# Attention in a hybrid diffusion block: who normalises the probabilities, and who splits weights and turns queries

## The chip, the core and the metric

The kernel runs on one core of one Trainium2 chip. Its engines take instructions each from a queue of its own, in order: TensorE (matmuls; PE in the profile, PEld for its weight loads), VectorE (DVE), ScalarE (ACT), GpSimd (POOL), and SyncE (SP), which only issues DMAs here. The metric is the device time of one execution in microseconds, lower is better.

## The reference

One layer over 512 latent tokens of width 1024 with 256 context tokens. What matters for the change is the attention: 16 query heads in 4 groups, each group with one key and value head of 64 columns. A block of 128 queries sees at most three blocks of 128 latent keys, all 256 context keys and one sink logit, in one softmax.

```python
qx = apply_axial_rope(qx.reshape(B, L, N_HEADS, HEAD_DIM), rope_cos, rope_sin)
...
s_loc = jnp.einsum('bqhgd,bshd->bhgqs', qn, kn).astype(jnp.float32) * ATTN_SCALE
s_ctx = jnp.einsum('bqhgd,bchd->bhgqc', qn, k_ctx).astype(jnp.float32) * ATTN_SCALE
s_loc = jnp.where(valid, s_loc, NEG_INF)
probs = jax.nn.softmax(jnp.concatenate([s_loc, s_ctx, sink_b], axis=-1), axis=-1)
...
return (jnp.einsum('bhgqs,bshd->bqhgd', p_loc, vn)
        + jnp.einsum('bhgqc,bchd->bqhgd', p_ctx, v_ctx))
```

The rotary step is `t1*cos - t2*sin`, `t2*cos + t1*sin` on pairs of columns. Beside the attention the layer has a pooling mixer, sigmoid gates, an output projection and a mixture of 32 experts (top 4 of them for each token), whose weights are most of what the kernel reads.

## The kernel before

All float32 products run as three matmuls of rounded halves. A tensor x is split into hi (x rounded, made by a copy on ScalarE) and lo = x - hi (a subtraction), and x*y becomes hi*hi + lo*hi + hi*lo. The subtraction for a weight is called a **weight difference** here, that for the transposed probabilities a **probability difference**.

The stages are: adaptive norm and key/value projections (to about 105 us), the attention (to about 396 us), pooling mixer, branch projections, output projection and routing (to about 650 us), and the experts, 32 of them with twelve weight pieces of 1 MB each, to the end.

The attention stage is written out by hand in the order in which each engine is to work. It goes over 16 **units** (4 groups x 4 query blocks; unit 0 starts at 118 us), each of six **slots** k = 0 to 5. In a slot:

- TensorE makes the scores of head k (S, two buffers in PSUM), transposes block k of the previous unit's probabilities (tp, two buffers), multiplies an older block with the values (pv), and fills up with `stream()`: 22 projection tiles of 24 matmuls (fps; six query tiles and sixteen gate tiles).
- ScalarE copies the transposed block to ph (`b_hi`, line 529), takes the exponential of head k-1 (`a_exp`, line 518; es of line 520 for the sink), normalises, and rounds weights (`s_split`, line 696).
- VectorE makes the probability difference pl = tp - ph (`b_lo`, line 533), the row maximum of head k (`a_max`, lines 513, 514), and in slots 2 and 4 the reciprocals of two heads at a time (`a_rec`, lines 501, 502).

`a_norm(U, k - 2)` (line 504) multiplies a head's probabilities with the reciprocal of their sum. Heads 0 and 2 follow right on the reciprocal in slots 2 and 4, heads 1 and 3 come in slots 3 and 5. Odd heads are normalised by ScalarE (line 507), even ones by VectorE (line 509). A unit's probabilities are 128 x 512 or 128 x 640 for each head.

Small pieces of work wait in the list `lazy` and are taken out one or two in a slot (`run_lazy(LZN[k])`), after the slot's main work: the output difference, the query's f13 (shuffle, two products, sum) and the query differences. A weight tile is rounded in two halves of 128 x 512 when the tile before it is at its 4th and 10th matmul; the two weight differences `f()` of a tile (line 699) run on GpSimd at once. When the second of a pair is done, the load of the next pair but one is issued. `stream()` doesn't begin a tile before both its differences are in the program.

The rotary step of four tiles ahead of the stage (`roped`, line 206; the last two are the queries of group 0) has one product on GpSimd and one product and the sum on VectorE. The six query tiles of the stage (`q_epi`) have both products and the sum on GpSimd (lines 613, 616, 619).

GpSimd and VectorE also share a third kind of work, **w_ada work**: a conditioning vector times a weight, ten column pieces in the units 0 to 7, 9 and 11. GpSimd does half of a piece in four instructions (lines 633, 635), VectorE the other half in eight running sums of 128 x 128 (lines 640, 642).

Of the kernel before, what the change touches and what calls it, by code (L numbers as in the profile page):

```python
# [10 lines left out]
F32 = mybir.dt.float32  # L11
# [4 lines left out]
AF = mybir.ActivationFunctionType  # L16
ALU = mybir.AluOpType
# [4 lines left out]
L = 512  # L22
# [46 lines left out]
def body(ctx, tc, x, c, cx, c_ctx, w_ada, b_ada, norm1_g, norm2_g, w_in, b_in, attn_sink, w_pool,  # L69
# [4 lines left out]
    pe, dve, act, pool = nc.tensor, nc.vector, nc.scalar, nc.gpsimd  # L74
# [122 lines left out]
    rope = slot("17a", [P, 2 * L], F32, "rope")  # L197
# [8 lines left out]
    def roped(pt, off, m, nm, t=None, t2=None):  # L206
        if t is None:
            t, t2 = wb([P, L], F32, "rope_t"), wb([P, L], F32, "rope_s")
        act.activation(t, pt, AF.Identity, bias=bcol(off, m), scale=1.0)
        dve.stream_shuffle(t2, t, swap)  # L210
        pool.tensor_mul(t, t, rope[:, 0:L])
        dve.tensor_mul(t2, t2, rope[:, L:])
        dve.tensor_add(t, t, t2)
        return t
# [288 lines left out]

    def a_norm(U, h):
        den, prob, W = U["den"], U["prob"], U["W"]
        if h % 2:
            act.activation(prob[:, h, 0:W], prob[:, h, 0:W], AF.Copy, scale=den[:, h:h + 1])
        else:
            dve.tensor_scalar(prob[:, h, 0:W], prob[:, h, 0:W], den[:, h:h + 1], None, op0=ALU.mult)

    def a_max(U, h, S):
        hd, W, nmh = GRP * U["g"] + h, U["W"], U["nm"][:, h:h + 1]
# [79 lines left out]
    def q_epi(g, m):  # L592
        def epi(pt):
            st = {}

            def f0():
                st["t"] = wb([P, L], F32, "rope_t")
                act.activation(st["t"], pt, AF.Identity, bias=bcol(OQ, 2 * g + m), scale=1.0)  # L598
                lazy.insert(0, f13)
                due.extend([(cnt[0] + 4, lambda: f5(0)), (cnt[0] + 5, lambda: f5(1))])  # L600

            def f13():
                f1()
                f2()
                f3()
                f4()

            def f1():
                st["t2"] = wb([P, L], F32, "rope_s")
                dve.stream_shuffle(st["t2"], st["t"], swap)  # L610

            def f2():
                pool.tensor_mul(st["t"], st["t"], rope[:, 0:L])

            def f3():
                pool.tensor_mul(st["t2"], st["t2"], rope[:, L:])

            def f4():
                pool.tensor_add(st["t"], st["t"], st["t2"])

            def f5(par):
                hd = 2 * m + par
                r = slice(par * 64, par * 64 + 64)
                ro = slice(64 - par * 64, 128 - par * 64)
                act.copy(qs_[g][r, hd, :], st["t"][r])
                lazy.insert(min(1, len(lazy)), lambda: dve.tensor_sub(qs_[g][ro, hd, :], st["t"][r],
                                                      qs_[g][r, hd, :].bitcast(F32)))
            post.insert(0, f0)
        return epi
# [57 lines left out]
    def s_split(i, part):  # L687
        if i >= len(tiles):
            return
        r, m, _ = tiles[i]  # L690
        if part == 0:
            wsp[i] = (hw([P, KT, P], F32R, "whi"), hw([P, KT, P], F32R, "wlo"))
        k = slice(4 * part, 4 * part + 4)
        hi, lo = wsp[i]
        src = raws[r][:, k, m * P:(m + 1) * P]
        act.copy(hi[:, k], src)

        def f():
            pool.tensor_sub(lo[:, k], src, hi[:, k].bitcast(F32))  # L699
            if part == 1 and m == 1:  # L700
                s_load(r + 2)
            wdone[i] = wdone.get(i, 0) + 1
        f()

    def stream():
        for i, (r, m, epi) in enumerate(tiles):
# [29 lines left out]
    with tc.manual_schedule():  # L736
# [23 lines left out]
        st = stream()  # L760
# [990 lines left out]
```

## Time and profile before

| what | value |
|---|---|
| median of 3 runs | 1830.98 us (1830.45 to 1831.39) |
| the profiled execution | 1827.51 us, its span 1825.7 us |
| TensorE busy | 1715.2 us, 94% of the span |
| VectorE busy | 1606.9 us, 88% |
| ScalarE busy | 1138.6 us, 62% |
| GpSimd busy | 411.6 us, 23% |
| DMA | 506.13 MB, 277 GB/s over the span |

The shares are means over stages that are bound by different things, so they don't tell what a change in one stage is worth. The views of stretches, groups and single units below are read for that. A duration in the profile holds the time in which an instruction has started but stands blocked; an idle gap before it is listed apart, with what ended it. Durations of neighbours overlap by about a tenth of a microsecond, so the distance from start to start is what an engine pays.

### The profile page before, as it was taken

To read this page: it belongs to the slowest core of one execution; us is meant where nothing else is said; L and a number is where in the kernel's file an instruction comes from. 1 tells how busy PE (TensorE), PEld (TensorE's weight loads), DVE (VectorE), ACT (ScalarE), POOL (GpSimd) and SP (SyncE) were. 2 spreads that over 40 slices of the span, in tenths; PEclk is the share of its full clock that TensorE was granted. 3 is DMA by queue.
4 is the path that set the end of the run, shared out by engine and by line. 5 is a ranking of instruction groups with operands and counts; after the bars stand their busy time and mean duration, and the time that the engine had idled before them with its cause. 6 is when DMAs were issued, how large, how long until landed. Compare 5 with 4: busy or idle time off the path is not lost. (4 is left out here: it accounts for less than half of the span.)

```text
span 1825.7 us, 22699 instructions
## 1 busy us (share of the span) xinstructions
PE 1715.2 (94%) x8398; PEld 1277.2 (70%) x8398; DVE 1606.9 (88%) x1691; ACT 1138.6 (62%) x1209; POOL 411.6 (23%) x260
## 2 busy tenths in 40 slices
PE   5888889999999899999999999999999999999994
PEld 3767777877779767776766777777777777777763
DVE  5589998848886789998999999999999999999994
ACT  5456666763242367775766677677667777776762
POOL 0055445222441011424411111211111121112001
PEclk9998999999999899999999999999999999999997
DMA  9223323234655799999999999999999999999972
GB/s 302 69 84 104 104 87 103 77 121 134 213 179 176 245 304 348 357 376 335 355 367 360 362 376 370 364 368 370 377 364 370 369 372 365 375 367 361 377 283 101
DMA packets 180380, 506.13 MB, mean 277 GB/s; under 512 B 12506, under 2 KB 69094, under 8 KB 180266
## 3 DMA queue, kind: packets, MB, share of 16 engines
q1 hardware_dynamic: 172170, 484.17, 72.7%
q0 software_dynamic: 8096, 20.48, 4.4%
q8 instruction: 67, 1.10, 0.2%
q14 instruction: 47, 0.39, 0.1%
HBM read 490.02 MB, written 22.69 MB: 281 GB/s over the span
## 5 line engine op out<-in xcount | busy, mean ns | idle before, releaser
L1555 DVE TENSOR_TENSOR mwl<-mw,mwh 128x2048 fp32r<-128x2048 f32 x384 | 873.3, 2283 | 37.1 <-PE gu L1285 29.4
L1548 ACT CAST mwh<-mw 128x2048 fp32r<-128x2048 f32 x384 | 727.3, 1911 | 258.6 <-PE dn L1285 118.8
L1285 PE MATMUL gu<-mwh,xT 128*96 128x512 f32 x2048 | 523.1, 398 | 3.0 <-DVE xT L125 2.7
L1285 PEld LDWEIGHTS gu<-mwh,xT 128*96 128x96 f32 x2048 | 327.1, 162 | 139.5 <-DVE xT L125 3.1
L1290 POOL DMA_INDIRECT acc<-y,igs x31 | 121.0, 3904 | 917.1 <-DVE y L1398 917.1
L1285 PE MATMUL gu<-mwl,xT 128*96 128x512 f32 x1024 | 280.1, 396 | 3.0 <-DVE mwl L1555 3.0
L1285 PE MATMUL dn<-mwh,aT 128*96 128x512 f32 x992 | 253.2, 397 | 0.0
L1285 PEld LDWEIGHTS gu<-mwl,xT 128*96 128x96 f32 x1024 | 166.0, 162 | 76.0 <-DVE mwl L1555 3.4
L1285 PEld LDWEIGHTS dn<-mwh,aT 128*96 128x96 f32 x992 | 155.4, 162 | 61.5
L1285 PE MATMUL dn<-mwl,aT 128*96 128x512 f32 x496 | 135.0, 394 | 0.0
L714 PE MATMUL fps<-hx,whi 128*128 128x512 f32 x352 | 124.3, 412 | 3.0 <-ACT rope_t L598 1.9
L1285 PEld LDWEIGHTS dn<-mwl,aT 128*96 128x96 f32 x496 | 79.9, 161 | 34.7
L1375 ACT ACTIVATE gs<-gs 96x1024 f32<-96x1024 f32 x32 | 34.0, 1062 | 88.8 <-DVE gs L1372 88.8
L1246 POOL DMA_INDIRECT xgb<-h2d,igs x31 | 79.9, 2577 | 40.8 <-DVE ltok L1180 16.7
L714 PEld LDWEIGHTS fps<-hx,whi 128*128 128x128 f32 x352 | 68.0, 195 | 19.0 <-ACT rope_t L598 3.0
L714 PE MATMUL fps<-hx,wlo 128*128 128x512 f32 x176 | 71.9, 409 | 0.8 <-POOL wlo L699 0.8
L518 ACT ACTIVATE prob<-S,nm 128x512 f32<-128x512 f32 (+1 forms) x64 | 47.8, 747 | 34.6 <-DVE nm L514 34.1
L533 DVE TENSOR_TENSOR pl<-tp,ph 128x512 fp32r<-128x512 f32 x72 | 49.2, 684 | 8.5 <-ACT ph L529 8.1
L525 PE MATMUL tp<-ident,prob 128*128 128x128 f32 x288 | 45.3, 281 | 11.3 <-DVE pl L533 11.2
L513 DVE TENSOR_REDUCE nm<-S 128x1 f32<-128x512 f32 (+1 forms) x64 | 47.9, 748 | 6.0 <-PE S L488 5.7
L1398 DVE SCALAR_TENSOR_TENSOR y<-dn,gts,g2r 96x512 f32<-96x512 f32 x64 | 44.9, 740 | 5.0 <-PE dn L1285 5.0
L529 ACT CAST ph<-tp 128x512 fp32r<-128x512 f32 x72 | 41.9, 584 | 5.0 <-PE tp L525 4.5
(418 smaller groups left out, 2564.0 us busy)
## 6 DMA issues: line engine op xcount, KB each, us to landing
mw<-in_w_gu_dram SPq DMA_DIRECT2D x256, 1024.0 KB
mw<-in_w_down_dram SPq DMA_DIRECT2D x128, 1024.0 KB
wada<-in_w_ada_dram SPq DMA_DIRECT2D x24, 1024.0 KB
gz<-gzt SPq DMA_DIRECT2D x16, 256.0 KB
sg<-gz SPq DMA_DIRECT2D x16, 256.0 KB
wo<-in_w_out_dram SPq DMA_DIRECT2D x4, 1024.0 KB
xt<-in_x_dram SPq DMA_DIRECT2D x2, 1024.0 KB
xh<-in_x_dram SPq DMA_DIRECT2D x4, 512.0 KB
```

What stands on the lines that cost most here:

```text
L513: dve.reduce_max(nmh, S[:, 0:W], axis=AX.X)
L518: act.activation(U["prob"][:, h, 0:W], S[:, 0:W], AF.Exp, bias=nmh, scale=SCALE, accum_out=U["den"][:, h:h + 1])
L525: pe.transpose(U["tp", j][:, h * P:(h + 1) * P], U["prob"][:, h, j * P:(j + 1) * P], ident)
L529: act.copy(U["ph", j], U["tp", j])
L533: dve.tensor_sub(pl, U["tp", j], U["ph", j].bitcast(F32))
L714: pe.matmul(pt, a[:, k, :], b(k), start=n == 0, stop=n == 3 * KT - 1)
L1246: pool.indirect_dma_start(out=xg, out_offset=None, in_=h2d, in_offset=bass.IndirectOffsetOnAxis(ap=ig, axis=0), bounds_check=L - 1, oob_is ...
L1285: pe.matmul(os_[j], lhs(a, k), b[:, k, j * L:(j + 1) * L], start=first and j not in seen, stop=last and j not in left)
L1290: pool.indirect_dma_start(out=acc, out_offset=bass.IndirectOffsetOnAxis(ap=iscat, axis=0), in_=y, in_offset=None, bounds_check=L - 1, oob_ ...
L1398: dve.scalar_tensor_tensor(st["y"][:, cs], st["dn"][n], st["gt"], g2r[0:CAP, cs], op0=ALU.mult, op1=ALU.mult)
L1548: act.copy(hi, raw)
L1555: eng.tensor_sub(lo, raw, hi.bitcast(F32))
```

## The change

It does three things. All four heads of a unit are normalised by ScalarE. The weight differences of `stream()` go from GpSimd to VectorE, and they no longer run at once but are put at the end of `lazy`. The rotary products and sums go from GpSimd to VectorE. The w_ada work stays as it was.

```diff
--- before.py
+++ after.py
@@ -208,7 +208,7 @@
             t, t2 = wb([P, L], F32, "rope_t"), wb([P, L], F32, "rope_s")
         act.activation(t, pt, AF.Identity, bias=bcol(off, m), scale=1.0)
         dve.stream_shuffle(t2, t, swap)
-        pool.tensor_mul(t, t, rope[:, 0:L])
+        dve.tensor_mul(t, t, rope[:, 0:L])
         dve.tensor_mul(t2, t2, rope[:, L:])
         dve.tensor_add(t, t, t2)
         return t
@@ -503,10 +503,7 @@
 
     def a_norm(U, h):
         den, prob, W = U["den"], U["prob"], U["W"]
-        if h % 2:
-            act.activation(prob[:, h, 0:W], prob[:, h, 0:W], AF.Copy, scale=den[:, h:h + 1])
-        else:
-            dve.tensor_scalar(prob[:, h, 0:W], prob[:, h, 0:W], den[:, h:h + 1], None, op0=ALU.mult)
+        act.activation(prob[:, h, 0:W], prob[:, h, 0:W], AF.Copy, scale=den[:, h:h + 1])
 
     def a_max(U, h, S):
         hd, W, nmh = GRP * U["g"] + h, U["W"], U["nm"][:, h:h + 1]
@@ -610,13 +607,13 @@
                 dve.stream_shuffle(st["t2"], st["t"], swap)
 
             def f2():
-                pool.tensor_mul(st["t"], st["t"], rope[:, 0:L])
+                dve.tensor_mul(st["t"], st["t"], rope[:, 0:L])
 
             def f3():
-                pool.tensor_mul(st["t2"], st["t2"], rope[:, L:])
+                dve.tensor_mul(st["t2"], st["t2"], rope[:, L:])
 
             def f4():
-                pool.tensor_add(st["t"], st["t"], st["t2"])
+                dve.tensor_add(st["t"], st["t"], st["t2"])
 
             def f5(par):
                 hd = 2 * m + par
@@ -696,11 +693,11 @@
         act.copy(hi[:, k], src)
 
         def f():
-            pool.tensor_sub(lo[:, k], src, hi[:, k].bitcast(F32))
+            dve.tensor_sub(lo[:, k], src, hi[:, k].bitcast(F32))
             if part == 1 and m == 1:
                 s_load(r + 2)
             wdone[i] = wdone.get(i, 0) + 1
-        f()
+        lazy.append(f)
 
     def stream():
         for i, (r, m, epi) in enumerate(tiles):
```

What this does to the order is seen in unit 4. VectorE, from the first reciprocal (rec: add of den and es, reciprocal) to the second, before (pl is the probability difference, nm the row maximum, prob the probabilities):

```order
L501 TENSOR_TENSOR den_1674<-den_1674,es_1676 128x2
L502 RECIPROCAL den_1674<-den_1674 128x2
L509 TENSOR_SCALAR prob_1673<-prob_1673,den_1674 128x512
L533 TENSOR_TENSOR pl_1784<-tp_1738,ph_1780 128x512
L513 TENSOR_REDUCE nm_1675<-S_1767 128x1
L514 TENSOR_SCALAR nm_1675<-nm_1675,nsink_92 128x1
L640 TENSOR_SCALAR wada2_1652<-wada2_1652,sil_103 128x128
L533 TENSOR_TENSOR pl_1803<-tp_1773,ph_1799 128x512
```

and after:

```order
L501 TENSOR_TENSOR den_1673<-den_1673,es_1675 128x2
L502 RECIPROCAL den_1673<-den_1673 128x2
L530 TENSOR_TENSOR pl_1783<-tp_1738,ph_1779 128x512
L510 TENSOR_REDUCE nm_1674<-S_1766 128x1
L511 TENSOR_SCALAR nm_1674<-nm_1674,nsink_92 128x1
L696 TENSOR_TENSOR wlo_1763<-ws__1287,whi_1762 128x512
L637 TENSOR_SCALAR wada2_1651<-wada2_1651,sil_103 128x128
L530 TENSOR_TENSOR pl_1803<-tp_1772,ph_1799 128x512
```

Line 509 is gone from behind the reciprocal, so that the probability difference follows it at once; a weight difference stands in front of the w_ada product of the next slot.

ScalarE in the same part of unit 4, from the copy of the second transposed block on, before (ph is the copy of a transposed block, whi a rounded weight half):

```order
L529 CAST ph_1746<-tp_1712 128x512
L518 ACTIVATE prob_1673,den_1674<-S_1706,nm_1675 128x512
L520 ACTIVATE es_1676<-sink_91,nm_1675 128x1
L696 CAST whi_1762<-ws__1222 128x512
L529 CAST ph_1780<-tp_1738 128x512
L518 ACTIVATE prob_1673,den_1674<-S_1732,nm_1675 128x512
L520 ACTIVATE es_1676<-sink_91,nm_1675 128x1
L507 ACTIVATE prob_1673<-prob_1673,den_1674 128x512
L529 CAST ph_1799<-tp_1773 128x512
```

and after:

```order
L526 CAST ph_1746<-tp_1712 128x512
L515 ACTIVATE prob_1672,den_1673<-S_1706,nm_1674 128x512
L517 ACTIVATE es_1675<-sink_91,nm_1674 128x1
L506 ACTIVATE prob_1672<-prob_1672,den_1673 128x512
L693 CAST whi_1762<-ws__1287 128x512
L526 CAST ph_1779<-tp_1738 128x512
L515 ACTIVATE prob_1672,den_1673<-S_1732,nm_1674 128x512
L517 ACTIVATE es_1675<-sink_91,nm_1674 128x1
L506 ACTIVATE prob_1672<-prob_1672,den_1673 128x512
L526 CAST ph_1799<-tp_1772 128x512
```

The normalisation of head 0 now stands in front of the rounded weight and of the third ph; before, ScalarE's first normalisation of the unit was head 1's, one exponential later.

VectorE in the last rotary chain ahead of unit 0, from the query differences of the first query tile to those of the second, before:

```order
L443 TENSOR_TENSOR qs_946<-rope_t_947,qs_946 64x512 x2
L210 STREAM_SHUFFLE rope_s_963<-rope_t_962 128x512
L212 TENSOR_TENSOR rope_s_963<-rope_s_963,rope_93 128x512
L213 TENSOR_TENSOR rope_t_962<-rope_t_962,rope_s_963 128x512
L443 TENSOR_TENSOR qs_946<-rope_t_962,qs_946 64x512 x2
L513 TENSOR_REDUCE nm_977<-S_980 128x1
```

and after:

```order
L443 TENSOR_TENSOR qs_946<-rope_t_947,qs_946 64x512 x2
L696 TENSOR_TENSOR wlo_959<-ws__800,whi_958 128x512
L210 STREAM_SHUFFLE rope_s_963<-rope_t_962 128x512
L211 TENSOR_TENSOR rope_t_962<-rope_t_962,rope_93 128x512
L212 TENSOR_TENSOR rope_s_963<-rope_s_963,rope_93 128x512
L213 TENSOR_TENSOR rope_t_962<-rope_t_962,rope_s_963 128x512
L696 TENSOR_TENSOR wlo_959<-ws__800,whi_958 128x512
L443 TENSOR_TENSOR qs_946<-rope_t_962,qs_946 64x512 x2
L510 TENSOR_REDUCE nm_977<-S_980 128x1
```

The product of line 211 has come over from GpSimd, and two weight differences stand around the chain.

## Rows read from the trace of the kernel before

**Rows 1.** Stretches: busy PE, PEld, DVE, ACT, POOL; TensorE's clock; DMA share; GB/s.

```profile
118.00:264.00 146.00, 124.11 (x668) 101.56 (x669) 138.90 (x257) 91.13 (x204) 83.14 (x66) 0.94 0.28 93
277.00:326.00 49.00, 44.32 (x258) 36.13 (x257) 44.13 (x86) 34.54 (x76) 26.37 (x22) 1.00 0.29 97
326.00:376.00 50.00, 50.00 (x305) 43.13 (x304) 38.47 (x86) 39.56 (x91) 11.85 (x9) 1.00 0.18 64
700.00:750.00 50.00, 50.00 (x233) 35.31 (x232) 49.29 (x36) 35.50 (x24) 10.16 (x3) 1.00 0.99 358
```

**Rows 2.** VectorE groups, 118 to 264 us: busy us, mean ns | idle before.

```profile
L642 DVE SCALAR_TENSOR_TENSOR wada<-wada,sil 128x128 f32<-128x128 f32 x54 | 34.5, 639 | 1.2
L501 DVE TENSOR_TENSOR den<-den,es 128x2 f32<-128x2 f32 x16 | 9.1, 571 | 0.8 <-ACT es L520 0.8
L509 DVE TENSOR_SCALAR prob<-prob,den 128x640 f32<-128x640 f32 x8 | 8.9, 1114 | 0.3
L509 DVE TENSOR_SCALAR prob<-prob,den 128x512 f32<-128x512 f32 x8 | 6.3, 784 | 0.3
L626 DVE TENSOR_TENSOR qs<-rope_t,qs 64x512 fp32r<-64x512 f32 x8 | 8.2, 1025 | 0.2
```

**Rows 3.** The same view, 277 to 326 us.

```profile
L642 DVE SCALAR_TENSOR_TENSOR wada<-wada,sil 128x128 f32<-128x128 f32 x12 | 6.1, 505 | 0.3
L501 DVE TENSOR_TENSOR den<-den,es 128x2 f32<-128x2 f32 x6 | 3.3, 552 | 0.5 <-ACT es L520 0.5
L509 DVE TENSOR_SCALAR prob<-prob,den 128x640 f32<-128x640 f32 x4 | 3.9, 982 | 0.1
L509 DVE TENSOR_SCALAR prob<-prob,den 128x512 f32<-128x512 f32 x2 | 2.4, 1188 | 0.1
```

**Rows 4.** Single lines, whole span: duration ns min/median/max, first and last start us.

```profile
L642 DVE SCALAR_TENSOR_TENSOR wada<-wada,sil x70: 334/352/1991, 132.0 to 328.0; 128x128 f32<-128x128 f32 x70
L501 DVE TENSOR_TENSOR den<-den,es x32: 143/160/1273, 121.6 to 376.7; 128x2 f32<-128x2 f32 x32
L533 DVE TENSOR_TENSOR pl<-tp,ph x72: 672/683/693, 140.2 to 388.8; 128x512 fp32r<-128x512 f32 x72
L626 DVE TENSOR_TENSOR qs<-rope_t,qs x12: 686/751/1686, 148.5 to 326.8; 64x512 fp32r<-64x512 f32 x12
L212 DVE TENSOR_TENSOR rope_s<-rope_s,rope x2: 693/693/693, 106.4 to 112.4; 128x512 f32<-128x512 f32 x2
```

**Rows 5.** GpSimd's weight differences (line 699) in the two stretches.

```profile
118.00:264.00 146.00, 30.68 (x22) 0.94 0.28 93
277.00:326.00 49.00, 9.41 (x8) 1.00 0.29 97
```

**Rows 6.** GpSimd's w_ada work, 118 to 264 us: line 633, then line 635.

```profile
118.00:264.00 146.00, 15.73 (x8) 0.94 0.28 93
...
118.00:264.00 146.00, 20.95 (x24) 0.94 0.28 93
```

**Rows 7.** VectorE, last rotary chain ahead of unit 0: start us, us.

```profile
112.35 0.69 DVE L212 TENSOR_TENSOR rope_s<-rope_s,rope 128x512 f32<-128x512 f32 x1
114.23 1.76 DVE L213 TENSOR_TENSOR rope_t<-rope_t,rope_s 128x512 f32<-128x512 f32 x1 [1.19 <-POOL rope_t L211]
```

**Rows 8.** Unit 4 in order of time: VectorE's rows, then ScalarE's.

```profile
198.75 0.17 DVE L502 RECIPROCAL den<-den 128x2 f32<-128x2 f32 x1
200.76 0.68 DVE L533 TENSOR_TENSOR pl<-tp,ph 128x512 fp32r<-128x512 f32 x1
...
197.22 0.61 ACT L529 CAST ph<-tp 128x512 fp32r<-128x512 f32 x1
199.01 0.72 ACT L507 ACTIVATE prob<-prob,den 128x512 f32<-128x512 f32 x1 [0.32 <-DVE den L502]
199.63 0.57 ACT L529 CAST ph<-tp 128x512 fp32r<-128x512 f32 x1
```

**Rows 9.** Waits of VectorE, 111 to 396 us: us in total, times, longest.

```profile
DVE pl L533 <- ACT ph L529: 8.1, 12, 1.7
```

## The prediction

> **What bounds the kernel now.** I read the profile from the outside in: first busy time by stretch, then the VectorE groups of the stretches the change touches, then one unit of the attention in order of time. The attention stage runs from 118 us, where unit 0 begins, to about 396 us. In its units 0 to 7 (118 to 264 us) and 9 to 11 (277 to 326 us) the busiest engine is VectorE: 138.9 of 146 us and 44.1 of 49 us, 95% and 90%, with TensorE at 85% and 90% and ScalarE at 62% and 70%. In units 12 to 15 (326 to 376 us) it turns round: TensorE is busy all 50 us, VectorE 77%, ScalarE 79% [rows 1]. So there are 195 us in which a microsecond of VectorE is worth about a microsecond, and 50 us in which it is worth nothing. What the attention gains or loses goes through to the end: the later part moves weights at a DMA share of 0.99 with 358 GB/s [rows 1], against 0.18 to 0.29 in the attention, and its loads start as the buffers of earlier stages come free, so a shift of this stage shifts all that follows.
>
> The second thing to see is that VectorE isn't 95% busy with its own work. The running sums of line 642 have a median of 352 ns but a mean of 639 ns in units 0 to 7, and the two-element addition of line 501 has 160 against 571 ns [rows 2, 4]. The probability differences of line 533, just as wide but with one input in PSUM, go from 672 to 693 ns over all 72 of them [rows 4]. So instructions whose operands all lie in SBUF sit blocked behind a GpSimd instruction, and those that read PSUM don't.
>
> **The change part by part.** All sums are made in the profiled execution (1827.5 us, span 1825.7); that is 3.5 us under the median of 1830.98, so I add the difference to the median.
>
> 1. VectorE loses its half of the normalisations: 8.9 + 6.3 us in units 0 to 7 and 3.9 + 2.4 us in units 9 to 11 [rows 2, 3]: -21.5 us, blocked time included.
>
> 2. Blocking given back. Of the other instructions, lines 642, 501 and 626 lose 54 x (0.639 - 0.352) = 15.5, 16 x (0.571 - 0.160) = 6.6 and 8 x (1.025 - 0.686) = 2.7 us in units 0 to 7, and lines 642 and 501 lose 12 x (0.505 - 0.352) = 1.8 and 6 x (0.552 - 0.160) = 2.4 us in units 9 to 11 [rows 2 to 4]: 29.0 us. GpSimd keeps only the w_ada work, lines 633 and 635: 15.7 + 21.0 of its 83.1 us in units 0 to 7 [rows 1, 6]; 56% of its time leaves. By that share 0.56 x 29 = 16 us come back; at most all 29. I take 25, near the upper end, because smaller groups that are blocked too are left out of the 29, and because the first two w_ada runs no longer stand behind weight differences in GpSimd's queue and can run before unit 0. -25 us, from -16 to -29.
>
> 3. VectorE takes over 22 + 8 weight differences [rows 5] and three operations for each of six rotary tiles, 48 instructions of 128x512. An unblocked multiplication of this kind took 693 ns [rows 4]: 48 x 0.69 = +33.1 us. In the 326 to 376 us stretch TensorE covers the rest.
>
> 4. These 48 read SBUF twice, so what is left on GpSimd can block them. Eight of its ten w_ada runs, four instructions each, take 36.7 us in units 0 to 7 [rows 6], so all ten some 46 us of the 195, at 1.15 us an instruction; hit with a chance of 0.24 and held for half of one, the 48 lose 48 x 0.24 x 0.57 = 6.5 us, and nothing where VectorE waits anyway. I take +4, from 0 to 6.5.
>
> The Trainium skill (SBUF - State Buffer, Who interferes with whom) says that a VectorE instruction with two SBUF inputs contends with GpSimd reads, that the one that started first keeps the shared pair for its whole length, and that an instruction with one SBUF input outside a 2-port mode doesn't contend. The trace agrees (line 533 never above 693 ns, line 642 up to 1991). By that rule term 4 is there; if the moved differences were as immune as line 533 is, the sum would be 4 us lower.
>
> VectorE's own load in the 195 us thus goes down by 21.5 + 25 - 33.1 - 4 = 9.4 us.
>
> 5. The new wait. This is where the forecast is decided. Head 0 and head 2 are now normalised on ScalarE, in the very slot in which VectorE makes their reciprocal, and behind them in ScalarE's queue stands the copy of the next transposed block (line 529), for which VectorE's next probability difference (line 533) waits. In unit 4 of before, the reciprocal starts at 198.75 us and VectorE needs the next copy at 200.76; ScalarE had made it at 197.22, before the reciprocal was there [rows 8]. After the change it can't: ScalarE stands still until the reciprocal is done, then normalises (0.62 us from one start to the next in unit 4, for 512 columns), then copies (0.57) [rows 8], with about 0.1 us for two handovers: VectorE gets its input 1.3 us after its reciprocal. In some units a weight copy of half a microsecond stands between (the order of unit 4 shows it); in others VectorE has a weight difference of 0.69 us to fill the hole, in unit 4 none. So the hole after the first reciprocal is 0.6 to 1.9 us. After the second one VectorE has its own work queued (w_ada products, differences, 0.7 to 1.4 us), so that hole is 0 to 1.0. Before, VectorE waited on this copy 12 times for 8.1 us in the whole stage [rows 9]. From 0.6 to 2.9 us a unit, I take 1.5, since the first hole is open nearly everywhere and the second seldom. Unit 0 has no probability differences, so ten units of the VectorE-bound stretches count: +15 us, from 6 to 29.
>
> 6. Start of the stage. In the last rotary chain before unit 0 VectorE waits 1.19 us for GpSimd's product and then its addition takes 1.76 us instead of 0.69, blocked by a weight difference [rows 7]. With all three operations in a row, 112.35 + 2 x 0.70 + 0.69 = 114.4 us instead of 115.99: -1.5 us, from 0 to -2, since ScalarE's casts come next.
>
> 7. The TensorE-bound units. ScalarE's 39.6 of 50 us [rows 1] takes eight more normalisations of some 0.75 us: 45.6, 91%. It has to wait for reciprocals as well. I take half a microsecond a unit, +2 us, from 0 to 5.
>
> Where the weight differences stand in the queue costs nothing: TensorE's wait for GpSimd before a second weight half becomes a wait for VectorE that an earlier probability difference has already met in all but the first tiles. The weight loads are issued behind the second difference, a slot or two later, with a whole pair of tiles still in hand.
>
> Sum: -9.4 + 15 - 1.5 + 2 = +6.1 us. Forecast: **1837 us**, slower by 0.3%.
>
> **The rivals.** (a) The relief passes through, and the kernel gets faster. That is one mechanism: between reciprocal and next difference VectorE always has more than the 1.3 us of work that ScalarE needs. Then the hole is 0.4 us a unit and term 7 is nothing: -9.4 - 1.5 + 4 = -7, that is 1824 us. For it speaks that ScalarE is only 62% busy where VectorE binds [rows 1]; against it, that in the order of unit 4 nothing at all stands there. It decides below about 0.9 us of hole a unit, where the sum crosses zero. The Trainium skill (Perfetto Trace Analysis, Optimizing Scalar/DVE Operations) says that a saturated VectorE may hand work to ScalarE, and that moves between VectorE and GpSimd might not help since they share a port. If the exchange with GpSimd gave nothing either way, -21.5 - 1.5 + 4 = -19 would make 1812 us; but terms 2 to 4 of the rows make that exchange 12 us dearer, so of this rival's chance I give it 0.04.
>
> (b) Both halves cancel: with holes of about 0.5 to 1.2 us a unit, 1831 us within 3.7. That needs only a slightly cheaper handover than mine, or w_ada blocking that falls into the holes.
>
> (c) ScalarE becomes the bound in the TensorE-bound units too, and GpSimd's remaining work blocks the 48 new instructions in full: -21.5 - 16 + 33.1 + 6.5 + 25 + 5 - 1 = +31, 1862 us. Against it: 9% of ScalarE are still free there.
>
> (d) The moved work isn't on VectorE at all, or the normalisations still alternate: the order rules that out.
>
> **How the numbers follow.** Differences within 0.2% (3.7 us) can't be told from none here. Forecast (+3.7 to +20 us) 0.50; rival (a) 0.22; (b) 0.24; (c) 0.04. Faster 0.22, same 0.24, slower 0.54. The ends of the unknown costs together would be about -13 and +36 us; two in ten are left out at 1823 and 1851. The likeliest case alone is 1835 to 1851.
>
> **What would show it.** Lines 642 and 501 with means near 400 and 250 ns confirm term 2. A new row in the waits, probability difference on ScalarE's copy, of 15 to 20 us in all (8.1 now), and ScalarE's normalisation waiting on the reciprocal 25 times or more confirm term 5; if both stay under 8 us, (a) is right. VectorE under 90% with TensorE no busier in units 1 to 7 means the holes are real. I am wrong if units 0 to 7 take less than 140 us, or if units 12 to 15 grow by more than 4 us, or if the later stages don't shift by what the attention does.

## The result: slower by 1.0%

| | before | after |
|---|---|---|
| median of 5 runs each, in one comparison | 1830.45 us (1827.59 to 1831.39) | 1847.89 us (1847.62 to 1850.55) |
| ratio, 95% interval | | 1.0102, 1.0088 to 1.0117 |
| span of the profiled execution | 1825.7 us | 1846.1 us |
| VectorE busy, GpSimd busy, whole span | 1606.9, 411.6 us | 1598.7, 313.4 us |

The forecast was 1837.0 us, with a range of 1823 to 1851. The direction and the range hold; the step is 17.4 us between the medians, not 6.1, and 20.4 us between the two profiled spans, by which the trace is read below. In the changed kernel the lines behind line 506 have moved up by three: the probability difference is line 530 there, ph 526, the row maximum 510, the running sums 639, the normalisation 506, GpSimd's w_ada work 630 and 632. One of the six executions of kernel e5 below took 2158.09 us at a granted clock of 0.745, and its time is the median of the other five.

Below are the stretches that [rows 1] has of before, now of the changed kernel: units 0 to 7, units 9 to 11, units 12 to 15, and 50 us of the experts. The columns are the same (stretch, its length, busy PE, PEld, DVE, ACT, POOL, clock, DMA share, GB/s).

```profile
121.80:268.00 146.20, 122.90 (x667) 99.72 (x668) 120.37 (x274) 101.09 (x220) 28.79 (x24) 0.95 0.28 90
283.00:337.70 54.70, 45.91 (x254) 37.05 (x253) 43.31 (x91) 38.64 (x83) 9.88 (x8) 0.97 0.26 87
337.70:392.40 54.70, 52.80 (x311) 43.32 (x310) 38.57 (x86) 42.83 (x96) 0.00 (x0) 1.00 0.17 58
720.00:770.00 50.00, 50.00 (x233) 35.29 (x232) 49.29 (x36) 35.34 (x25) 10.85 (x3) 1.00 0.99 364
```

VectorE is no longer the bound of units 0 to 7: 120.4 us of 146 where it had 138.9 [rows 1]. Yet the stretch is as long as it was. Some 18 us of work have turned into as much idle time. Units 9 to 11 grew from 49.2 to 54.7 us although VectorE has a little less to do, and units 12 to 15 from 49.6 to 54.7. The waits of the stretch from 85 to 420 us show what ended that idle time (total us, times, longest; first VectorE, then ScalarE, then TensorE):

```profile
DVE pl L530 <- ACT ph L526: 37.1, 35, 2.5
...
ACT prob L506 <- DVE den L502: 36.8, 32, 5.1
ACT qs L442 <- DVE rope_t L213: 11.1, 2, 8.7
...
PE tp L522 <- DVE pl L530: 17.1, 11, 4.4
PE fps L711 <- ACT gzt L584: 6.5, 8, 1.7
```

The first row is that of [rows 9], which had 8.1 us in 12 waits. The next one says why: ScalarE's normalisation now waits 32 times for VectorE's reciprocal, twice in each of 16 units (8 times before, 7.0 us). Unit 4 shows one such turn in order of time (VectorE's two rows, then ScalarE's three):

```profile
199.91 0.17 DVE L502 RECIPROCAL den<-den 128x2 f32<-128x2 f32 x1
201.92 0.69 DVE L530 TENSOR_TENSOR pl<-tp,ph 128x512 fp32r<-128x512 f32 x1 [1.84 <-ACT ph L526]
...
200.17 0.72 ACT L506 ACTIVATE prob<-prob,den 128x512 f32<-128x512 f32 x1 [1.62 <-DVE den L502]
200.80 0.60 ACT L693 CAST whi<-ws__1287 128x512 fp32r<-128x512 f32 x1
201.31 0.58 ACT L526 CAST ph<-tp 128x512 fp32r<-128x512 f32 x1
```

ScalarE stands still for 1.62 us until the reciprocal is there, and then VectorE stands still for 1.84 us until ScalarE has normalised, rounded a weight half and copied ph. In [rows 8] the copy had been made before the reciprocal started. Each engine waits for the other in turn; this is called the **handshake** below.

A second loss lies ahead of unit 0, where the forecast had put a gain. GpSimd's first two w_ada runs start at 93.8 us, since no weight difference and no rotary product stands before them in GpSimd's queue any more; in the kernel before the first one starts at 120.5. GpSimd's rows of the changed kernel, then VectorE's beside them:

```profile
93.78 1.91 POOL L630 TENSOR_TENSOR wada<-wada,sil 128x1024 f32<-128x1024 f32 x1 [78.02 <-DMA wada<-in_w_ada_dram]
95.77 4.17 POOL L632 TENSOR_TENSOR wada<-wada 128x512 f32<-128x512 f32 x3
99.89 2.35 POOL L630 TENSOR_TENSOR wada<-wada,sil 128x1024 f32<-128x1024 f32 x1
102.32 3.09 POOL L632 TENSOR_TENSOR wada<-wada 128x512 f32<-128x512 f32 x3
...
93.87 2.37 DVE L213 TENSOR_TENSOR kb<-kb 128x512 f32<-128x512 f32 x1
96.16 2.31 DVE L125 TENSOR_TENSOR wlo<-wq__146,whi 128x1024 fp32r<-128x1024 f32 x1
98.39 1.22 DVE L426 TENSOR_TENSOR kkx<-kb,kkx 64x512 fp32r<-64x512 f32 x1
...
100.49 2.03 DVE L426 TENSOR_TENSOR kkc<-kb,kkc 64x256 fp32r<-64x256 f32 x1
...
106.86 1.23 DVE L125 TENSOR_TENSOR wlo<-wq__146,whi 128x1024 fp32r<-128x1024 f32 x1
```

In the kernel before, the same VectorE instructions go like this, with nothing on GpSimd between 93.4 and 103.2 us:

```profile
94.23 0.68 DVE L213 TENSOR_TENSOR kb<-kb 128x512 f32<-128x512 f32 x1
94.83 1.21 DVE L125 TENSOR_TENSOR wlo<-wq__146,whi 128x1024 fp32r<-128x1024 f32 x1
...
97.36 0.42 DVE L426 TENSOR_TENSOR kkc<-kb,kkc 64x256 fp32r<-64x256 f32 x1
...
100.51 1.23 DVE L125 TENSOR_TENSOR wlo<-wq__146,whi 128x1024 fp32r<-128x1024 f32 x1
```

Every one of them has two inputs in SBUF, and blocked ones take up to five times as long (2.03 against 0.42 us). The second weight of the queries is split 6.35 us later (106.86 against 100.51), and unit 0 starts at 121.8 us instead of 118.0: the rotary chains in between give 2.5 us back. The last of them, from its shuffle to the end of its addition, takes 4.42 us before and 2.79 in the changed kernel (the first row is of before, where the addition of [rows 7] ends at 115.99):

```profile
111.57 0.75 DVE L210 STREAM_SHUFFLE rope_s<-rope_t 128x512 f32<-128x512 f32 x1
...
117.05 0.74 DVE L210 STREAM_SHUFFLE rope_s<-rope_t 128x512 f32<-128x512 f32 x1
...
119.15 0.69 DVE L213 TENSOR_TENSOR rope_t<-rope_t,rope_s 128x512 f32<-128x512 f32 x1
```

### The profile page after: what moved, and what is told of

It reads as the page before. It is cut to its first block, busy times and chain, and to the rows that moved or that the text cites. A ratio compares the mean times of both kernels' runs of the same rounds, so it can differ in the third digit from the quotient of the medians.

```text
span 1846.1 us, 22667 instructions
## 1 busy us (share of the span) xinstructions
PE 1719.4 (93%) x8398; PEld 1275.8 (69%) x8398; DVE 1598.7 (87%) x1725; ACT 1157.8 (63%) x1241; POOL 313.4 (17%) x194
## 5 line engine op out<-in xcount | busy, mean ns | idle before, releaser
L1287 POOL DMA_INDIRECT acc<-y,igs x31 | 116.5, 3759 | 929.7 <-DVE y L1395 929.7
L530 DVE TENSOR_TENSOR pl<-tp,ph 128x512 fp32r<-128x512 f32 x72 | 49.5, 688 | 37.4 <-ACT ph L526 37.1
L1243 POOL DMA_INDIRECT xgb<-h2d,igs x31 | 72.7, 2347 | 40.1 <-DVE ltok L1177 16.0
L506 ACT ACTIVATE prob<-prob,den 128x512 f32<-128x512 f32 (+1 forms) x64 | 49.4, 774 | 36.8 <-DVE den L502 36.8
L630 POOL TENSOR_TENSOR wada<-wada,sil 128x1024 f32<-128x1024 f32 x10 | 20.2, 2018 | 256.3 <-DMA wada<-in_w_ada_dram 143.1
```

The costliest lines, as they stand in the source:

```text
L530: dve.tensor_sub(pl, U["tp", j], U["ph", j].bitcast(F32))
L1243: pool.indirect_dma_start(out=xg, out_offset=None, in_=h2d, in_offset=bass.IndirectOffsetOnAxis(ap=ig, axis=0), bounds_check=L - 1, oob_is ...
L1287: pool.indirect_dma_start(out=acc, out_offset=bass.IndirectOffsetOnAxis(ap=iscat, axis=0), in_=y, in_offset=None, bounds_check=L - 1, oob_ ...
```

## The experiments

**Theory.** Three things make up the loss: the handshake of reciprocal, normalisation and ph in the units; its effect in the TensorE-bound units; and the blocked start. **Rivals.** It is the amount of work on ScalarE, wherever it stands; or it is the work that VectorE took over; or the early w_ada runs only move their blocked time. The table has all kernels of the study by stretch, in us. A unit begins with its first row maximum on VectorE, and unit 15 is counted to its last. "Tiles end" is the last matmul of the projection tiles, with which the attention stage ends, and "rest" is from there to the end of the span.

| kernel | unit 0 starts | units 0-7 | units 9-11 | units 8, 12-15 | tiles end | rest | median |
|---|---|---|---|---|---|---|---|
| before | 118.0 | 145.5 | 49.2 | 62.7 | 394.4 | 1431.3 | 1830.45 |
| after | 121.8 | 146.1 | 54.7 | 69.7 | 411.2 | 1434.9 | 1847.89 |
| e1 norm only | 118.1 | 151.5 | 53.1 | 68.6 | 410.2 | 1431.3 | 1843.30 |
| e2 weight differences only | 120.5 | 141.7 | 48.3 | 64.6 | 393.4 | 1432.5 | 1828.68 |
| e3 rotary only | 116.0 | 145.3 | 52.9 | 62.7 | 395.8 | 1430.3 | 1831.71 |
| e4 late norm | 122.7 | 136.9 | 49.1 | 65.0 | 392.5 | 1430.0 | 1823.84 |
| e5 gate | 118.0 | 147.0 | 54.5 | 69.7 | 407.9 | 1435.1 | 1844.42 |
| e6 late norm and gate | 119.0 | 136.1 | 49.1 | 64.9 | 388.0 | 1429.9 | 1819.76 |
| e7 alternating norm | 121.5 | 137.7 | 48.7 | 64.3 | 390.6 | 1430.7 | 1825.51 |
| e8 before, late norm | 119.6 | 138.9 | 45.8 | 64.3 | 387.5 | 1431.2 | 1821.51 |
| e9 head 0 late | 122.7 | 137.3 | 51.7 | 64.7 | 395.3 | 1430.3 | 1832.89 |
| e10 head 2 late | 122.9 | 145.6 | 52.0 | 68.9 | 407.4 | 1431.7 | 1838.19 |
| e11 late norm, rotary on GpSimd | 120.6 | 132.4 | 47.6 | 64.9 | 384.4 | 1433.1 | 1820.50 |
| e12 late norm, weight differences on GpSimd | 117.7 | 141.3 | 53.5 | 64.3 | 395.8 | 1433.3 | 1830.04 |

In the comparisons of e1 to e12 the kernel before had medians of 1828.99 to 1829.34 us, in that of the changed kernel 1830.45; distances from the changed kernel across comparisons are good to that 1.5 us. The start of unit 0 varies by up to 1.7 us between profiles of kernels whose work ahead of it is the same (before, e1 and e8: 118.0 to 119.6; after, e4, e7, e9 and e10: 121.5 to 122.9). The stretches are of one profiled execution each, of 1827.42 us for e9 and 1840.87 us for e10. The rest, too, differs by up to 5.2 us between kernels, for a reason that stays open, so a gain in the time isn't all a gain in the attention.

### e4 and e5: the two losses, one at a time

e4 keeps all normalisations on ScalarE and moves only their place:

```diff
-                if A and 2 <= k < GRP + 2:
-                    a_norm(A, k - 2)
+                if A and k in (3, 5):
+                    a_norm(A, k - 3)
+                    a_norm(A, k - 2)
```

> The changed kernel, with all four normalisations still on ScalarE, but heads 0 and 1 in slot 3 and heads 2 and 3 in slot 5, one slot behind their reciprocals for heads 0 and 2. ScalarE does the same work. Theory (ScalarE stands still for the reciprocal, the copy of the transposed block stands behind it, VectorE waits for the copy): ScalarE's wait for den falls from 36.8 us to under 8, VectorE's wait for ph from 37.1 to under 18, and the time falls by 12 to 22 us, to 1826 to 1836. Rival 1 (it is the added ScalarE work itself, 32 normalisations, not where they stand): the time stays within 3 us of the changed kernel's 1847.9. Rival 2 (two normalisations in the last slot make the next unit's transposes late): above 1848, with TensorE's transposes waiting on ScalarE's normalisation, for which they do not wait now.

Measured: 1823.84 us, ratio to before 0.9974 (0.9964 to 0.9984), 24 us under the changed kernel. ScalarE's wait for the reciprocal has fallen from 36.8 to 1.4 us, and VectorE's wait for ph is

```profile
DVE pl L530 <- ACT ph L526: 13.3, 19, 1.9
```

Unit 4, VectorE and then ScalarE, shows the turn without the handshake:

```profile
196.44 0.17 DVE L502 RECIPROCAL den<-den 128x2 f32<-128x2 f32 x1
196.52 0.67 DVE L530 TENSOR_TENSOR pl<-tp,ph 128x512 fp32r<-128x512 f32 x1
...
195.52 0.60 ACT L526 CAST ph<-tp 128x512 fp32r<-128x512 f32 x1
...
196.85 1.35 ACT L506 ACTIVATE prob<-prob,den 128x512 f32<-128x512 f32 x2
198.08 0.60 ACT L526 CAST ph<-tp 128x512 fp32r<-128x512 f32 x1
```

The copy of ph stands ahead of the normalisations, and the difference follows the reciprocal at once. ScalarE does the same work as in the changed kernel, so the amount of it isn't the cause; both rivals of this run fall. The gain is a little over the 12 to 22 us that were expected: the tiles end 18.7 us earlier, and 4.9 us more are gained in the rest.

e5 holds GpSimd's first w_ada runs back by a copy of one column that needs the last rotary result:

```diff
         q_out(1, qr1)
+        pool.tensor_copy(gate, qr1[:, 0:1])
```

> The changed kernel with one tiny copy (128 x 1) on GpSimd that reads the last rotary result ahead of unit 0, so that the first two w_ada runs of GpSimd cannot start at 93.8 us but only after the last rotary step. Theory (these runs block VectorE's differences and rotary steps ahead of unit 0): VectorE's key differences between 96 and 107 us are back to 0.42 to 0.69 us each, unit 0 starts near 117 instead of 121.85 us, and the time falls by 3 to 5 us, to 1843 to 1845. Rival (the blocked time only moves into units 0 and 1, where VectorE is then blocked for as long): unit 0 starts earlier, but unit 2 starts where it does now, and the time stays within 1.5 us of 1847.9.

Measured: 1844.42 us, ratio 1.0082 (1.0069 to 1.0095), 3.5 us under the changed kernel. GpSimd's first w_ada run now starts at 113.95 us, VectorE's key differences and the weight split have their old durations, and unit 0 starts at 118.0:

```profile
97.26 0.42 DVE L426 TENSOR_TENSOR kkc<-kb,kkc 64x256 fp32r<-64x256 f32 x1
...
100.41 1.22 DVE L125 TENSOR_TENSOR wlo<-wq__146,whi 128x1024 fp32r<-128x1024 f32 x1
...
114.03 4.03 DVE L443 TENSOR_TENSOR qs<-rope_t,qs 64x512 fp32r<-64x512 f32 x2
...
113.40 0.58 POOL L757 COPY gate<-rope_t 128x1 f32<-128x1 f32 x1 [97.57 <-DVE rope_t L213]
113.95 1.90 POOL L631 TENSOR_TENSOR wada<-wada,sil 128x1024 f32<-128x1024 f32 x1
```

Units 0 to 7 pay 0.9 us of it back (147.0 against 146.1), and unit 2 starts at 155.7 us where the changed kernel has 159.0, so the rival, that the blocked time only moves, falls. But the gate opens one step too early. The run that it holds back starts beside the last two query differences (line 443), which take 4.03 us where the kernel before has 1.41. These 2.6 us are why unit 0 starts no earlier than before, although the rotary chain ends 2.7 us earlier (113.33 against 115.99).

### e6 and e7: both, and the normalisations taken back

> Both of the above: normalisations one slot later and the first w_ada runs of GpSimd held back. Theory: the two losses lie in different stretches and add up, so that the gain is the sum of the two single gains within 3 us: 1821 to 1832, under the kernel before (1830.5) if the late normalisation gives 15 us or more. Rival (something else, such as the differences and rotary steps that VectorE took over, still costs some 10 us): 1835 to 1842 even with both gone.

Measured: 1819.76 us, ratio 0.9954 (0.9941 to 0.9967). The single gains of 24.0 and 3.5 us add up to 27.5; together they give 28.1, as expected, and the time is 1.2 us under the range. This kernel is faster than before and after; e8 and e11 below are within 2 us of it, and their intervals overlap with its own.

e7 undoes the first part of the change alone (`if h % 2` is back in `a_norm`).

> The changed kernel with the normalisations alternating again (odd heads ScalarE, even heads VectorE), so only the weight differences and the rotary steps are moved. Theory: VectorE's wait for ph is back under 12 us (37.1 in the changed kernel), VectorE does 22 x 0.7 = 15 us more in units 0 to 7 and 9 to 11 of which some 22 us of holes are filled: 1838 to 1845. Rival (the moved VectorE work is what costs, and the normalisations on ScalarE relieved it): the time rises by 8 to 15 us, to 1856 to 1863.

Measured: 1825.51 us, ratio 0.9980 (0.9971 to 0.9989), 22.4 us under the changed kernel. VectorE's wait for ph is 5.6 us. The two moves of work, by themselves and in spite of the late start, make the kernel faster by 0.2%; the normalisations on ScalarE, in the slots of their reciprocals, make it slower. The time is 12.5 us under the range that was expected, and under that of the rival too. The expectation counted VectorE-bound units only, with 7 us: they give 14.4, units 8 and 12 to 15 give 5.4 (69.7 to 64.3), and the rest 4.2.

### e1, e2, e3: each part alone, on the kernel before

> The kernel before with one part of the change alone: all normalisations on ScalarE, each in the slot it had. Theory (head 0 and head 2 wait on ScalarE for a reciprocal of the same slot): ScalarE waits over 25 us for den and VectorE over 25 us for ph, which eats the 21.5 us that VectorE gives away: 1838 to 1852, slower than the 1829 of before. Rival (in the crowded VectorE of before the relief counts in full and the waits fill holes that are there anyway): 1812 to 1826.

Measured: 1843.30 us, ratio 1.0085 (1.0071 to 1.0099). The waits are those of the changed kernel, and larger:

```profile
DVE pl L530 <- ACT ph L526: 44.7, 39, 2.5
...
ACT prob L506 <- DVE den L502: 41.0, 32, 3.1
```

> The kernel before with the weight differences alone moved to VectorE, at the end of lazy. Theory: VectorE pays 30 x 0.68 = 20.5 us in units 0 to 7 and 9 to 11 and gets most of the blocked time back (30.7 + 9.4 us of GpSimd's work are gone, the mean of line 642 falls from 639 to under 480 ns): 1825 to 1834. Rival (the blocked time was GpSimd's rotary and w_ada work, not the differences): line 642 stays over 550 ns and the time is 1840 to 1850.

Measured: 1828.68 us, ratio 0.9996 (0.9987 to 1.0005), no difference. Line 642 fell to a mean of 429 ns in units 0 to 7 (639 before), so the blocked time does come back, and it pays for the work that VectorE takes over; some 2 us of it are lost at the start of unit 0 (e11, which begins like it, has 120.6). TensorE also waits 6.5 us for weight differences that come late from `lazy`, where the changed kernel has 0.3 us.

> The kernel before with the rotary products and sums alone moved to VectorE. The weight differences stay on GpSimd ahead of its w_ada runs, so that these still start after unit 0 begins. Theory: unit 0 starts 1 to 2 us before 118 us, VectorE pays 18 x 0.7 = 12.6 us and gets 5 to 12 us of blocked time back: 1827 to 1835. Rival (the rotary work lies on VectorE's chain and costs in full): 1837 to 1843.

Measured: 1831.71 us, ratio 1.0016 (1.0007 to 1.0025). Unit 0 starts at 116.0 us, 2.0 us earlier than before, and at 117.7 in e12, 1.9 us earlier than in e8, from which e12 differs in the same way. Of this only 0.6 us lie in the last rotary chain (3.82 us from shuffle to sum, 4.42 before), since its first product is now blocked in its turn (1.72 us); the rest comes from the chains ahead of it. The loss lies in units 9 to 11 (52.9 against 49.2 us). The three parts alone sum to 14.1 - 0.5 + 2.6 = 16.2 us; the change has 17.4.

### e8: the relief without the handshake

Only `a_norm` and its slots differ from the kernel before (the diffs of e1 and e4 together).

> The kernel before with all normalisations on ScalarE, but heads 0 and 1 in slot 3, heads 2 and 3 in slot 5, and nothing else moved. Against the run with the normalisations alone it differs only in where ScalarE's work stands. Theory: no wait for den, VectorE keeps the relief of 21.5 us less 3 to 10 us that TensorE then takes: 1808 to 1820, faster than before by more than any other kernel here. Rival (VectorE is then bound by blocked time all the more, since GpSimd keeps its 83 us, or TensorE binds at once): 1821 to 1829.

Measured: 1821.51 us, ratio 0.9959 (0.9946 to 0.9973), 21.8 us under e1 with the same instructions on the same engines. It is 1.5 us short of the range of the theory and in that of the rival: the running sums are blocked more than ever while the weight differences stay on GpSimd, with a mean of 698 ns from 115 to 268 us, against 629 before in the same window (count | busy us, mean ns | idle):

```profile
L639 DVE SCALAR_TENSOR_TENSOR wada<-wada,sil 128x128 f32<-128x128 f32 x56 | 39.1, 698 | 1.2
```

### e9 and e10: which of the two handshakes

```diff
-                if A and 2 <= k < GRP + 2:
-                    a_norm(A, k - 2)
+                for h in {3: (0, 1), 4: (2,), 5: (3,)}.get(k, ()):
+                    if A:
+                        a_norm(A, h)
```

e10 has `{2: (0,), 3: (1,), 5: (2, 3)}` in the same place.

> The changed kernel, in which only head 0's normalisation is moved, into slot 3 ahead of head 1's; head 2 stays in the slot of its reciprocal. In the changed kernel VectorE's hole before the third probability difference of a unit is 19.5 us in all, open in 15 of 15 units, and before the fifth 9.6 us, in 7 of 8. Theory: the hole before the third difference goes, the one before the fifth stays, and the time is 12 to 18 us under the changed kernel: 1830 to 1836. Rival (either wait alone is enough to hold the units, since the next one takes over what was gained): within 6 us of 1847.9.

> The changed kernel, in which only head 2's normalisation is moved, into slot 5 ahead of head 3's; head 0 stays in the slot of its reciprocal. Theory: the hole before the third probability difference stays near 19 us and that before the fifth falls below 5; the time is 5 to 10 us under the changed kernel: 1838 to 1843, and the two single gains (this and the one with head 0 moved) add up to the 24 us of both together. Rival (the second hole costs nothing, because VectorE has work of its own queued after the second reciprocal, as the prediction says of it): 1846 to 1849.

Measured: e9 1832.89 us, ratio 1.0023 (1.0012 to 1.0035); e10 1838.19 us, ratio 1.0045 (1.0032 to 1.0059). Against the changed kernel that is 15.0 and 9.7 us, 24.7 together, where both at once gave 24.0. VectorE's hole before the third probability difference is gone in e9 (9.4 us are left before the fifth), and that before the fifth falls to 2.3 us in e10 (19.5 are left before the third). Not all of the time lies there: the tiles end 15.9 us earlier in e9, but only 3.8 us earlier in e10, and 3.2 us of e10's gain are in the rest. VectorE's waits for ph in e9, then in e10:

```profile
DVE pl L530 <- ACT ph L526: 17.7, 20, 1.9
```

```profile
DVE pl L530 <- ACT ph L526: 30.0, 31, 2.5
```

Head 0's turn costs more; head 2's costs some 4 us in the attention, and the remainder of its 9.7 us isn't shown to be its own. Units 12 to 15 take 53.7 us with head 0's turn alone (e10) and 50.6 with head 2's (e9), against 54.7 with both and 50.6 with neither (e4): the loss in the TensorE-bound units is head 0's.

### e11 and e12: which of the moved work is worth moving

Both have late normalisations. e11 leaves all rotary work on GpSimd, e12 the weight differences.

> Normalisations on ScalarE one slot later, weight differences on VectorE as in the changed kernel, but all rotary products and sums on GpSimd as before. GpSimd's rotary product of the last chain ahead of unit 0 again holds back its first w_ada runs. Theory: VectorE saves 18 x 0.7 us of rotary work and pays part of it as blocked time (mean of line 639 between 400 and 480 ns, against 382 with the rotary work on VectorE): 1815 to 1822, near the 1819.8 of the kernel with both parts moved and the gate. Rival (what is left on GpSimd blocks the moved weight differences in full): 1823 to 1830.

> Normalisations on ScalarE one slot later, rotary steps on VectorE as in the changed kernel, but the weight differences on GpSimd at once as before. Theory: the weight differences are what blocks VectorE most, so line 639 stays above 550 ns in units 0 to 7, the start of unit 0 is near 116 us (no w_ada run ahead of it), and the time is that of the late normalisation alone (1821.5) plus the 2.5 us that the rotary steps alone cost: 1821 to 1827. Rival (the rotary steps gain once VectorE has the normalisations off its hands): 1813 to 1820.

Measured: e11 1820.50 us, ratio 0.9957 (0.9943 to 0.9970); e12 1830.04 us, ratio 1.0000 (0.9991 to 1.0009). e11 came as expected. e12 missed by 3 us: the rotary steps on VectorE don't only cost their time. `f13` puts shuffle, products and sum on VectorE in one go, and with weight differences and w_ada work on GpSimd the products and the sum are blocked (1.40 to 2.27 us, against 0.69 in [rows 4]). VectorE's rows of unit 11 in e12, and TensorE's transposes that wait for the next probability difference behind them:

```profile
305.35 0.76 DVE L607 STREAM_SHUFFLE rope_s<-rope_t 128x512 f32<-128x512 f32 x1
306.15 1.40 DVE L610 TENSOR_TENSOR rope_t<-rope_t,rope 128x512 f32<-128x512 f32 x1
307.47 1.78 DVE L613 TENSOR_TENSOR rope_s<-rope_s,rope 128x512 f32<-128x512 f32 x1
309.28 2.27 DVE L616 TENSOR_TENSOR rope_t<-rope_t,rope_s 128x512 f32<-128x512 f32 x1
...
314.95 1.09 PE L522 MATMUL tp<-ident,prob 128*128 128x128 f32 x4 [4.21 <-DVE pl L530]
```

Over 85 to 420 us TensorE's wait for probability differences before a transpose is 20.0 us in e12 and 3.0 in e11 (8.2 in e8, which has all of that work on GpSimd, and 12.9 in e4, which has all of it on VectorE):

```profile
PE tp L522 <- DVE pl L530: 20.0, 7, 5.3
```

```profile
PE tp L522 <- DVE pl L530: 3.0, 6, 0.6
```

## Why the forecast had the direction right and the size wrong

The sum in the profiled execution, by the steps of the prediction (us):

| step | forecast | measured |
|---|---|---|
| 1 normalisations off VectorE | -21.5 | -21.5 |
| 2 blocked time given back | -25 (-16 to -29) | -34 |
| 3 moved work, unblocked | +33.1 (48 instructions) | +30.6 (45) |
| 4 its own blocked time | +4 (0 to 6.5) | +7 |
| 5 new idle time in units 0 to 7 and 9 to 11 | +15 (6 to 29) | +25 |
| units 0 to 7 and 9 to 11 together | +5.6 | +6.1 |
| 6 start of unit 0 | -1.5 (0 to -2) | +3.8 |
| 7 units 8 and 12 to 15 | +2 (0 to 5) | +7.0 |
| attention stage | +6.1 | +16.8 |
| rest of the kernel | 0 | +3.6 |

The measured terms 2 to 4 are VectorE's durations above the shortest of the same line and shape, summed over the units, in each of the two traces; term 5 is what VectorE's busy time went down by (19.1) plus what the units grew by. The terms overlap by a microsecond or two.

**Steps 1 to 5** come out at the right sum by luck: two errors of about 10 us cancel. Term 2 was too small: the running sums are wholly free again and the additions of line 501 nearly so, where means of 400 and 250 ns were named as the sign, and the smaller groups that the prediction left out of its 29 us give the rest (the first products of the w_ada pieces 3.3 us, the key differences 3.6). The rows answer to [rows 2] (units 0 to 7 of the changed kernel):

```profile
L639 DVE SCALAR_TENSOR_TENSOR wada<-wada,sil 128x128 f32<-128x128 f32 x54 | 19.0, 352 | 1.2
...
L623 DVE TENSOR_TENSOR qs<-rope_t,qs 64x512 fp32r<-64x512 f32 x8 | 5.5, 686 | 0.2
...
L610 DVE TENSOR_TENSOR rope_t<-rope_t,rope 128x512 f32<-128x512 f32 x4 | 4.9, 1215 | 0.1
...
L501 DVE TENSOR_TENSOR den<-den,es 128x2 f32<-128x2 f32 x16 | 3.1, 191 | 1.0 <-ACT es L517 0.9
```

(The prediction calls line 533 "just as wide" as line 642; it has 128x512 to 128x128, the width of the moved work, and no sum rests on it.) Term 4 is seen in the rotary product of line 610: 1215 ns instead of the 693 of [rows 4]; the weight differences, 15.1 us for 21 in units 0 to 7, were hit little. Term 5 was the right mechanism, in the place and the order that the prediction took from unit 4. Its first hole was priced from 0.6 to 1.9 us and is 1.84 in unit 4; it is open in 15 of 15 units before the third probability difference, 19.5 us in all and 12.8 in the ten units that the prediction counted. The second was said to open seldom and is open before the fifth difference in 7 of the 8 units that have five: 9.6 us, 6.3 in the ten units. That is the part of the handshake that was mis-sized, and the row of waits that was to be 15 to 20 us is 37.1. Of the 25 us of new idle time 20.7 are waits for ph; the other 4 have no term in the prediction. For terms 4, 5 and 7 rival (c), with a chance of 0.04, was nearer (6.5, 25 and 5); its 1862 us fail by the blocked time, -34 for its -16.

Rival (a), that the relief passes through, gave 1824 us. With the handshake taken away the relief does pass through: e4 has 1823.84. That the two numbers agree is luck, since e4 still starts unit 0 late; with the gate as well it is 1819.76 (e6). The rival's condition, enough work on VectorE to fill the hole, wasn't met, neither in the changed kernel nor in e4, which has no hole there.

**Step 6 came out with the wrong sign, by work that no term prices.** The rotary chain itself gained what was forecast: 1.6 us (4.42 to 2.79). What failed is a clause of step 2. The prediction saw that the first two w_ada runs "no longer stand behind weight differences in GpSimd's queue and can run before unit 0", and booked it as a gain under step 2. It didn't ask what VectorE does at that time: key differences and a weight split on the chain to unit 0, all with two inputs in SBUF. That held the chain up by 6.35 us, of which 2.5 came back. Holding the runs back gains 3.5 us of the time and 3.8 at unit 0 (e5). The Trainium skill (SBUF - State Buffer, Who interferes with whom) has the rule that two-input VectorE instructions contend with GpSimd's reads; the trace agrees (0.42 against 2.03 us, for a key difference). The prediction applied it to the units and not to the stretch into which the same GpSimd work moved.

**Step 7 was mis-sized.** Half a microsecond a unit was booked for units 12 to 15; "units 12 to 15 grow by more than 4 us" was named as a sign that the prediction is wrong, and they grew by 5.1. Unit 8, which stands in no term of the prediction, grew by 1.9, which makes the 7.0 us of the table. Idle time of VectorE was taken as free there. With the normalisations late the five units are back to 65.0 us, within 2.3 of before (e4), so the order of the queue costs 4.7 of the 7.0. How the delay reaches TensorE isn't shown. What stands behind ScalarE's wait isn't only ph but also the emptying of the projection tiles' PSUM (gzt), for which TensorE waits 6.5 us in the stage (0.7 before); yet in units 12 to 15 TensorE is idle for 1.9 us in all, and e10 has 53.7 us there with 2.0 us of that wait in the whole stage.

**The exchange between GpSimd and VectorE.** The Trainium skill (Perfetto Trace Analysis, Optimizing Scalar/DVE Operations) says that moves between VectorE and GpSimd might not help. e2 agrees: no difference. So do e8 and e11, which have the normalisations late and differ only in where the weight differences run: 1821.51 and 1820.50 us. But e12 and e4 differ in the same thing, with the rotary steps on VectorE, and there VectorE is better by 6.2 us (1830.04 to 1823.84), 3.3 of them in the rest. So the exchange pays where other work of VectorE would be blocked, such as the rotary steps of e12; room on VectorE alone isn't enough.

**What stays open.** The rest of the kernel behind the attention took 3.6 us more in the profile of the changed kernel, and 3.8 in e5, which has the same attention; in the other twelve kernels it lies between 1429.9 and 1433.3 us, whatever the length of the attention (e1, with tiles ending at 410.2, has 1431.3). In these two it is already there when the routing's first matmul (lgps) starts, 177.0 and 176.1 us behind the tiles' end, against 172.3 to 174.1 in the others. No run here tells what makes them differ. The prediction had taken the shift to go through unchanged and had named the contrary as a sign that it is wrong.

## What to carry to other kernels

Before work is handed from one in-order engine to another, look at what the receiver must wait for in that very place, and at what stands behind it in its queue: the same 32 normalisations on ScalarE cost 14 us in the slot of their reciprocal (e1) and gain 8 us one slot later (e8). With them late, the two other moves give nothing that can be told from none (e8 1821.51, e6 1819.76). When work leaves an engine's queue, what is left in it starts earlier; ask what that collides with there, and hold it back with a cheap dependency if need be (e5), past all of the work that it would block. An engine that is not the bound can still hold up the one that is: units 12 to 15 took 54.7 us with ScalarE's waits and 50.6 without them (e4).

## What the runs showed of the hardware beyond what was expected

A VectorE instruction with two SBUF inputs is blocked again and again while GpSimd works through a row of instructions: the eight between 93.87 and 105.97 us of the changed kernel took 12.2 us, the same eight of before 5.5. GpSimd isn't spared either: its three additions of line 632 took 4.17 us there, and 3.26 us in e5, where they run beside the start of unit 0.
